# Two K pairs of the output projection's first half change places

## The chip, the cores and the metric

The kernel runs on one core of one Trainium2 chip. The metric is the device time of one execution in microseconds (us), as the median of the runs; lower is better. TensorE (PE) multiplies matrices and loads its stationary operand in a separate instruction (PEld), VectorE (DVE) and ScalarE (ACT) do the elementwise work, GpSimd (POOL) helps in a few places, and SyncE (SP) issues most of the DMAs. PSUM has eight banks of 128x512 f32 in which matmuls add up.

## The reference, cut to what matters

Two layers, 256 tokens, width 2048. Each layer has a mixer and a SwiGLU block, both with a norm ahead and a norm behind and a residual. The mixer has two groups of eight heads, whose outputs stand side by side and go through one output projection:

```python
o_sb = stick_breaking_attention(q_sb, k_sb, v_sb)      # heads 0 to 7
o_sb = rms_norm(o_sb, sb_out_norm)
...
o_d = differential_attention(q1, q2, k1, k2, v_d, lam) # heads 8 to 15
o_d = rms_norm(o_d, diff_subln) * (1.0 - lam_init)
mix = jnp.concatenate([o_sb.reshape(b, s, SB_WIDTH), o_d.reshape(b, s, DIFF_V_WIDTH)], axis=-1)
return mix @ w_o
```

`mix` is 256 x 2048 and `w_o` is 2048 x 2048. The sum over the 2048 rows of `w_o` may be taken in any order.

## The kernel before, in words

**Splitting.** Every f32 operand is split into a rounded part `hi` and the rest `lo`. A product of two split operands is three matmuls, hi x hi, hi x lo and lo x hi, of 128x128 by 128x512, which all add into one PSUM bank (lines 629 to 631). ACT makes `hi` of a weight tile (line 330), DVE makes `lo` (line 340). A ring of six `hi` and six `lo` buffers holds the split weights, and a ring of four `raw` buffers holds what the DMA has brought (512 KB each).

**The weight stream.** All weights are laid out in DRAM in the order in which they are used, by `weight_order()`. Each entry is a tile of two K tiles (a "K pair", 256 rows of the weight) by 512 columns (a "column" c). SP fetches the entries in that order, and ACT and DVE split them four entries ahead of their use.

**The output projection.** K pair kp covers heads 2kp and 2kp+1: pairs 0 to 3 are the stick-breaking heads, pairs 4 to 7 the differential ones. Columns 0 and 1 are the first half, columns 2 and 3 the second. The first half takes the K pairs in the order `KP_O`, both columns of a pair behind each other:

```python
KP_O = (4, 5, 6, 7, 0, 1, 2, 3)                                      # line 34
order_o = [(c, kp) for kp in KP_O for c in (0, 1)]                   # line 108
...
for n, (c, kp) in enumerate(units[6:]):                              # line 1296
    ...
    run_until(lambda: mixed >= {2 * kp, 2 * kp + 1})                 # line 1303
    unit({t: accs[c, t] for t in range(NT)}, mix, ..., kp, ...)      # line 1304
```

Pairs 4 and 5 go through a form with seven products instead of eight (`sevens_alone`, line 1293), with pair 6 woven between; pair 7 and pairs 0 to 3 are plain `unit`s. One unit is one entry of the weight stream: two K tiles by two token halves by three matmuls, 12 matmuls. Behind the seven products, `pool.end_of_sums()` (line 1294) frees the room in which the stick-breaking results are later put.

**The attention beside it.** The attention is written as generators which run beside the projections. `tick()` advances a counter and lets every generator whose turn has come issue its next stage; a plain `yield` sleeps two ticks, `yield 1` one. Each `unit` ticks twice, once ahead of each of its K tiles. `run_until(done)` ticks without issuing any unit until `done` holds. Stick-breaking heads come in two groups of four heads; group 0 fills K pairs 0 and 1, group 1 fills pairs 2 and 3. `attend()` (line 744) goes through one group, two heads at a time: it multiplies the weights with the values (lines 758 to 760, PSUM tile `o_sb`), two ticks later it takes squares (line 710), two ticks later it normalizes into `on` (line 715), and after four more ticks it transposes `on` on PE (line 729, tile `oT_ps`, four transposes, two per head) and ACT and DVE write the split result `mix` (lines 731 and 734); then the heads enter the set `mixed`. Only one group may be between its products and its `on` at a time (`attending`), so that the two groups take turns: heads 0 and 1, heads 4 and 5, heads 2 and 3, heads 6 and 7. The transposes want one of three shared PSUM banks, and those of stick-breaking heads wait for `end_of_sums`.

**What sets the order of the queues.** The program issues in the order in which the code runs, and that order is a priority. A planner at compile time then makes each engine's queue from the priorities and its own estimate of when the operands are there: where an instruction is not ready by that estimate, a later one that is ready goes ahead. On the chip the queues run in the planned order.

**Behind it.** The second half takes columns 2 and 3 in the order `LATE_O` (pair 6 first, then pair 4 through the seven products with weights in buffers `V`), then a part in an order written out by hand leads into the SwiGLU block (PE tile `c`), which is most of the time.

Of the kernel before, what the change touches and what calls it, by code (L numbers as in the profile page):

```python
# [30 lines left out]
DEFER_ACT = 7  # L31
URGENT = 50
TAIL = 3
KP_O = (4, 5, 6, 7, 0, 1, 2, 3)
LATE_O = (6, 4, 0, 1, 5, 2)
LAST_O = (3, 7)
O_SEVEN = (4, 5)
# [51 lines left out]
def weight_order():  # L89
# [9 lines left out]
    for l in range(L):  # L99
# [7 lines left out]
        aside[lay["in"][PAIRS[-1][1], IN_LAST[1]]] = "v"  # L107
        order_o = [(c, kp) for kp in KP_O for c in (0, 1)]
        order_o += [(c, kp) for kp in LATE_O for c in (2, 3)] + [(c, kp) for c in (2, 3) for kp in LAST_O]
        lay["order_o"] = order_o  # L110
        for c, kp in order_o:
            lay["o"][c, kp] = queue_pair("w_o", l, kp, c)
            if c == 3 and kp in O_SEVEN:
                own.add(lay["o"][c, kp])
            if c == 1 and kp in KP_O[:2]:
                plain.add(lay["o"][c, kp])
        aside[lay["o"][1, KP_O[1]]] = "sums"
        for c in range(FF // CW):
# [61 lines left out]
def kernel(  # L180
# [435 lines left out]
    def run_until(done):  # L616
        while not done():
            tick()
# [396 lines left out]
    def mixer_in(pool, l, rs, xT, mix, mixed):  # L1015
# [7 lines left out]
        for n, cc in enumerate(PAIRS):  # L1023
# [60 lines left out]
            else:  # L1084
# [3 lines left out]
                if alone:  # L1088
# [9 lines left out]
                    kps = kps[3:]  # L1098
                    ahead = list(KP_O[:2])
                for j, kp in enumerate(kps):  # L1100
# [166 lines left out]
    for l in range(L):  # L1267
# [18 lines left out]
        units = plan[l]["order_o"][:16]  # L1286
        run_until(lambda: mixed >= {2 * kp + j for kp in KP_O[:3] for j in range(2)})

# [3 lines left out]

        sevens_alone(got, forms, mix, KP_O[:2], [plan[l]["o"][c, kp] for c, kp in units[:4]], w, units_between)
        pool.end_of_sums()
# [406 lines left out]
```

## Time and profile before

| what | value |
|---|---|
| median of the runs | 2179.39 us |
| all runs | 2178.74, 2184.57, 2179.39 us |
| profiled execution, its own time | 2180.22 us |
| its span (first to last instruction) | 2178.5 us |
| mean granted TensorE clock | 0.999 |

The profiled execution is 0.83 us above the median, and its span is 1.7 us shorter than its time. All stamps below are us from the start of that span. A row of the timeline reads: start, duration, engine, line, operation, what it writes `<-` what it reads, shape, number, and in brackets how long the engine had been idle and what ended that. The names drop the numbers of the buffers, so `mix_sb` is the split result of any stick-breaking pair, `mix_df` that of any differential pair. The output projection's first half is at 296 to 349 us in layer 0 and at 1380 to 1433 us in layer 1.

### The profile page before, as it was taken

The page shows a single profiled execution, that of the slowest core. Times are in us where ns is not written, and L with a number is a line of the kernel's source. Part 1 is how long each engine was busy: PE and PEld are TensorE (multiplying, and loading weights), DVE is VectorE, ACT ScalarE, POOL GpSimd, SP SyncE. Part 2 cuts the span into 40 slices and gives each one's busy share as a digit, 9 for nine tenths or more (in the row PEclk, how much of TensorE's full clock was granted, in tenths as well). Part 3 has the DMA queues.
Part 4 walks back from the last instruction along what each step waited for, and adds up shares of the span by engine and source line. Part 5 has one row for each costly group of instructions (what it writes and reads, how often), then busy time and mean ns, then how long its engine had stood idle before and what let it go on. Part 6 is the DMA issues. An engine that isn't in the chain of part 4 may idle for free.

```text
span 2178.5 us, 28781 instructions
## 1 busy us (share of the span) xinstructions
PE 2161.9 (99%) x9932; PEld 1778.3 (82%) x9932; DVE 1960.4 (90%) x2705; ACT 1414.4 (65%) x2113; POOL 246.5 (11%) x239
## 2 busy tenths in 40 slices
PE   9999999999999999999999999999999999999998
PEld 7888888888888888888878888888888888888886
DVE  7888977899999999999878888778999999999997
ACT  7666775765766666666665667757566666576664
POOL 2100000021221220000010000000212212200000
PEclk9999999999999999999999999999999999999999
DMA  8545446497887877767465564455978877767683
GB/s 324 194 165 200 161 171 199 156 307 230 248 260 225 232 234 233 224 228 253 146 242 174 179 206 155 171 179 184 294 232 253 257 224 237 232 218 241 203 269 99
DMA packets 140275, 470.44 MB, mean 216 GB/s; under 512 B 15952, under 2 KB 16976, under 8 KB 139616
## 3 DMA queue, kind: packets, MB, share of 16 engines
q1 hardware_dynamic: 121952, 436.03, 57.9%
q0 software_dynamic: 17600, 32.02, 8.9%
q8 instruction: 78, 1.28, 0.2%
q14 instruction: 69, 0.57, 0.1%
q10 hardware_dynamic: 576, 0.54, 0.1%
HBM read 460.14 MB, written 8.39 MB: 215 GB/s over the span
## 4 chain that ended last, share of the span: by engine, by line
PE 90%; DVE 5%; ACT 2%; DMA 2%; issue 2%; DVEq 0%; SPq 0%; ACTq 0%
PE c L1351 20%; PE in L1219 7%; PE in L1221 7%; PE in L1220 7%; PE dn L1582 4%; PE dn L1585 4%; PE dn L1583 4%; PE p L1220 3%; PE c L1219 2%; PE c L1220 2%; PE p L1221 2%; PE c L1221 2%; PE p L1219 2%; PE o L629 2%; PE o L631 2%; PE o L630 2%
## 5 line engine op out<-in xcount | busy, mean ns | idle before, releaser
L340 DVE TENSOR_TENSOR lo<-raw,hi 128x1024 fp32r<-128x1024 f32 x448 | 544.0, 1233 | 58.5 <-ACT hi L330 57.4
L330 ACT ACTIVATE hi<-raw 128x1024 fp32r<-128x1024 f32 x470 | 480.1, 1054 | 73.6 <-DMA raw<-in_weights_in_turn_dram 33.2
L1351 PE MATMUL c<-hi,xF 128*128 128x512 f32 x1344 | 364.4, 392 | 0.7 <-DVE xF L539 0.5
L1351 PEld LDWEIGHTS c<-hi,xF 128*128 128x128 f32 x1344 | 249.7, 188 | 53.3 <-ACT act L1469 1.9
L270 POOL DMA_DIRECT2D T<-in_weights_in_turn_dram x122 | 107.6, 882 | 1367.5 <-PE c L1351 541.0
L1351 PE MATMUL c<-lo,xF 128*128 128x512 f32 x672 | 207.4, 390 | 0.0
L302 ACT ACTIVATE Th<-T 128x512 fp32r<-128x512 f32 x122 | 77.2, 633 | 199.4 <-DVE T L313 198.4
L302 ACT ACTIVATE Th<-G 128x1024 fp32r<-128x1024 f32 x122 | 129.0, 1058 | 80.0 <-DVE G L314 78.6
L1582 PE MATMUL dn<-hi,jh 128*128 128x512 f32 x416 | 162.0, 389 | 0.0
L1583 PE MATMUL dn<-lo,jh 128*128 128x512 f32 x416 | 161.8, 389 | 0.0
L304 DVE TENSOR_TENSOR Tl<-G,Th 128x1024 fp32r<-128x1024 f32 x122 | 148.9, 1221 | 11.6 <-ACT Th L302 11.6
L304 DVE TENSOR_TENSOR lo<-T,hi 128x1024 fp32r<-128x1024 f32 x122 | 152.9, 1253 | 0.1
L330 ACT ACTIVATE hi<-G 128x1024 fp32r<-128x1024 f32 x122 | 128.9, 1056 | 36.5 <-DMA G<-in_weights_in_turn_dram 22.1
L314 DVE TENSOR_TENSOR G<-G,T 128x1024 f32<-128x1024 f32 x122 | 148.7, 1219 | 2.6 <-DVE T L313 0.9
L1351 PEld LDWEIGHTS c<-lo,xF 128*128 128x128 f32 x672 | 126.0, 188 | 26.4
L340 DVE TENSOR_TENSOR lo<-G,hi 128x1024 fp32r<-128x1024 f32 x104 | 126.8, 1219 | 10.1 <-ACT hi L330 9.9
L302 ACT ACTIVATE hi<-T 128x1024 fp32r<-128x1024 f32 x122 | 128.0, 1050 | 11.4 <-PE c L1221 8.3
L1585 PE MATMUL dn<-hi,jl 128*128 128x512 f32 x416 | 128.1, 389 | 0.0
L1219 PE MATMUL in<-hi,xT 128*128 128x512 f32 x316 | 125.9, 400 | 1.6 <-DVE xT L929 1.6
L1219 PE MATMUL in<-hi,xI 128*128 128x512 f32 x316 | 126.1, 400 | 0.0
L1220 PE MATMUL in<-lo,xI 128*128 128x512 f32 x316 | 123.5, 391 | 0.3 <-DVE lo L340 0.3
L1221 PE MATMUL in<-hi,xI 128*128 128x512 f32 x316 | 123.2, 391 | 0.0
(522 smaller groups left out, 5028.8 us busy)
## 6 DMA issues: line engine op xcount, KB each, us to landing
raw<-in_weights_in_turn_dram SPq DMA_DIRECT2D x482, 512.0 KB, 4.9
T<-in_weights_in_turn_dram SPq DMA_DIRECT2D x122, 512.0 KB, 5.3
G<-in_weights_in_turn_dram SPq DMA_DIRECT2D x122, 512.0 KB, 5.4
T<-in_weights_in_turn_dram POOLq DMA_DIRECT2D x122, 256.0 KB, 5.6
GU<-in_weights_in_turn_dram SPq DMA_DIRECT2D x48, 512.0 KB, 6.4
V<-in_weights_in_turn_dram SPq DMA_DIRECT2D x8, 512.0 KB, 5.3
away_ffn<-x SPq DMA_DIRECT2D x8, 512.0 KB, 7.2
xd<-away_ffn SPq DMA_DIRECT2D x8, 512.0 KB, 9.2
```

The lines of the kernel that those rows point to most:

```text
L302: nc.scalar.activation(h, w, AF.Copy)
L304: newest_rest[i] = nc.vector.tensor_tensor(out=l, in0=w, in1=h.bitcast(F32), op=ALU.subtract)
L314: nc.vector.tensor_tensor(out=g, in0=g, in1=t2.unsqueeze(1).to_broadcast([P, 2, CW]), op=ALU.add)
L330: nc.scalar.activation(hi, raw, AF.Copy)
L340: rest = nc.vector.tensor_tensor(out=lo, in0=raw, in1=hi.bitcast(F32), op=ALU.subtract)
L1219: nc.tensor.matmul(a, sh, hi, start=first, stop=False, skip_group_check=open_sums[0])
L1220: nc.tensor.matmul(a, sh, lo, start=False, stop=False, skip_group_check=open_sums[0])
L1221: return nc.tensor.matmul(a, sl, hi, start=False, stop=last, skip_group_check=open_sums[0])
L1351: nc.tensor.matmul(a, stat[part], w[j][:, kk, :], start=first and kk + n == 0, stop=last and kk == 1 and n == 2)
L1582: nc.tensor.matmul(accs[c, t], sh, hi[:, kk, :], start=first, stop=False, skip_group_check=open_sums[0])
L1583: nc.tensor.matmul(accs[c, t], sh, lo[:, kk, :], start=False, stop=False, skip_group_check=open_sums[0])
L1585: nc.tensor.matmul(accs[c, t], sl, hi[:, kk, :], start=False, stop=last, skip_group_check=open_sums[0])
```

## The change

K pairs 1 and 2 change places in `KP_O`:

```diff
-KP_O = (4, 5, 6, 7, 0, 1, 2, 3)
+KP_O = (4, 5, 6, 7, 0, 2, 1, 3)
```

`KP_O` is read in four ways. `weight_order()` lays out the weight stream by it, so the four entries of pairs 1 and 2 (two columns each) change places in DRAM too, in both layers. `units` (line 1286) is the same list. `KP_O[:2]` (pairs 4 and 5), `KP_O[:3]` (line 1287) and `KP_O[-1]` (pair 3, lines 1304 and 1305) are what they were. The order of the generators' stages and the second half's order are not touched.

## The prediction

> **What bounds the kernel now.** I read the totals of the page first, then TensorE's waits, then the stretches around the change, then the timeline of each engine there.
>
> ```profile
> span 2178.5 us, 28781 instructions
> PE 2161.9 (99%) x9932; PEld 1778.3 (82%) x9932; DVE 1960.4 (90%) x2705; ACT 1414.4 (65%) x2113; POOL 246.5 (11%) x239
> ...
> raw<-in_weights_in_turn_dram SPq DMA_DIRECT2D x482, 512.0 KB, 4.9
> ```
> ```profile
> PE p L1220 <- DVE Tl L304: 2.5, 3, 1.2
> ...
> PE oT_ps_sb L729 <- DVE on_sb L715: 1.5, 2, 0.9
> ```
> ```profile
> 330.00:350.00 20.00, 19.34 (x88) 15.61 (x87) 13.52 (x20) 9.13 (x15) 0.00 (x0) 1.00 0.59 203
> 1414.00:1434.00 20.00, 19.13 (x89) 15.56 (x88) 13.74 (x21) 9.48 (x15) 0.00 (x0) 1.00 0.58 203
> 540.00:700.00 160.00, 160.00 (x724) 132.71 (x722) 155.82 (x173) 106.88 (x122) 36.83 (x28) 1.00 0.82 248
> ```
>
> TensorE works for 2161.9 of 2178.5 us, so all its idle time together is 16.6 us. Of that, 1.5 us in two waits belongs to the output projection's first half, one in each layer: transposes of a stick-breaking result wait for `on`. The two stretches of 20 us hold nothing else that TensorE waits for (20 less 19.34 is 0.66, 20 less 19.13 is 0.87), VectorE is busy there for 13.5 and 13.7 us, ScalarE for 9.1 and 9.5. There TensorE alone sets the pace.
>
> The timeline of TensorE in layer 0 shows the place. A matmul's stamped duration overlaps the next, so prices are taken from start to start.
>
> ```profile
> 316.44 0.60 PE L729 MATMUL oT_ps_sb<-ident,on_sb 128*128 128x128 f32 x4
> 316.88 0.39 PE L758 MATMUL o_sb<-v,w_sb 128*128 128x128 f32 x2
> ...
> 320.73 0.39 PE L631 MATMUL o<-hi,mix_df 128*128 128x512 f32 x1
> 320.95 0.60 PE L729 MATMUL oT_ps_sb<-ident,on_sb 128*128 128x128 f32 x4
> 321.31 0.47 PE L629 MATMUL o<-hi,mix_df 128*128 128x512 f32 x1
> 321.62 0.39 PE L630 MATMUL o<-lo,mix_df 128*128 128x512 f32 x1
> ...
> 324.14 0.38 PE L758 MATMUL o_sb<-v,w_sb 128*128 128x128 f32 x2
> ...
> 330.70 0.39 PE L631 MATMUL o<-hi,mix_sb 128*128 128x512 f32 x1
> 330.94 0.60 PE L729 MATMUL oT_ps_sb<-ident,on_sb 128*128 128x128 f32 x4
> 332.13 0.41 PE L729 MATMUL oT_ps_sb<-ident,on_sb 128*128 128x128 f32 x2 [0.59 <-DVE on_sb L715]
> ...
> 336.85 0.38 PE L729 MATMUL oT_ps_sb<-ident,on_sb 128*128 128x128 f32 x2
> ...
> 340.52 0.39 PE L629 MATMUL o<-hi,mix_sb 128*128 128x512 f32 x1
> ...
> 349.36 0.39 PE L629 MATMUL o<-hi,mix_df 128*128 128x512 f32 x1
> ```
>
> I call the results A, B, C, D in the order in which their transposes appear: 316.44 (A), 320.95 (B), 330.94 (C), and D in two halves at 332.13 and 336.85. Counted in ticks from `end_of_sums` by the code: A's transposes and C's products come at tick 1 (316.44 and 316.88 stand together), B's transposes at tick 3, between the two units of pair 7, C's `on` and D's products at tick 5 (324.14), C's transposes and D's `on` at tick 9, D's transposes at tick 13. With the groups in turns A is pair 0, B pair 2, C pair 1, D pair 3. The units of pairs 7 and 0 use ticks 1 to 8. Their last matmul is at 330.70. Then the program wants pair 1, which is C, not yet in `mixed`: `run_until` issues tick 9 with no unit under it. TensorE transposes C, and all that stands ready next in its queue is C's own result, which ScalarE and VectorE have yet to write. The planner filled this hole with half of D's transposes, and D's `on` was not there:
>
> ```profile
> 320.80 0.69 DVE L715 TENSOR_TENSOR on_sb<-o_sb,ors_sb 128x512 f32<-128x512 f32 x1
> ...
> 323.12 0.48 DVE L734 SCALAR_TENSOR_TENSOR mix_sb<-oT_ps_sb,gains,mix_sb 128x256 fp32r<-128x256 f32 x1 [0.54 <-ACT mix_sb L731]
> ...
> 331.29 0.69 DVE L715 TENSOR_TENSOR on_sb<-o_sb,ors_sb 128x512 f32<-128x512 f32 x1
> ...
> 334.39 0.48 DVE L734 SCALAR_TENSOR_TENSOR mix_sb<-oT_ps_sb,gains,mix_sb 128x256 fp32r<-128x256 f32 x1 [0.55 <-ACT mix_sb L731]
> ...
> 340.89 0.48 DVE L734 SCALAR_TENSOR_TENSOR mix_sb<-oT_ps_sb,gains,mix_sb 128x256 fp32r<-128x256 f32 x1
> ```
>
> B, which is pair 2, was complete at 323.12 + 0.48 = 323.60, seven microseconds before the hole, and its 24 matmuls were queued behind pair 1.
>
> **The change part by part.** *The order on TensorE.* Pair 2's two units (24 matmuls) go ahead of pair 1's (24). The count stays. `run_until` finds pair 2 in `mixed` and issues nothing, so ticks 9 to 12 lie under pair 2's units and tick 13 under pair 1's first. C's transposes (tick 9) come at the same place as now, ahead of pair 2; D's (tick 13) come between pair 2 and pair 1. C's result then has pair 2's 24 matmuls to hide behind, and D's `on` (331.29 + 0.69 = 331.98) is there well before its transposes.
>
> *The sum for layer 0.* The 39 steps from 340.52 to 349.36 take 8.84 us, 0.2267 us a matmul. Four transposes between two matmuls cost what 320.73 to 321.62 takes, 0.89, less two steps of 0.2267: 0.44 us. From the last matmul of pair 0 to the first of the second half there are 73 steps and two groups of transposes: 73 x 0.2267 + 2 x 0.44 = 17.42 us. Now it takes 349.36 - 330.70 = 18.66 us. The gain is 1.24 us: the wait of 0.59, and the refilling behind it with D's transposes cut in two.
>
> ```profile
> 1414.33 0.39 PE L631 MATMUL o<-hi,mix_sb 128*128 128x512 f32 x1
> ...
> 1416.03 0.41 PE L729 MATMUL oT_ps_sb<-ident,on_sb 128*128 128x128 f32 x2 [0.87 <-DVE on_sb L715]
> ...
> 1433.01 0.39 PE L629 MATMUL o<-hi,mix_df 128*128 128x512 f32 x1
> ```
>
> *Layer 1* takes 1433.01 - 1414.33 = 18.68 us for the same work: 1.26 us. Together 2.50 us.
>
> *What is late next.* C is needed at 330.70 + 25 x 0.2267 + 2 x 0.44 = 337.25 and was complete at 334.39 + 0.48 = 334.87, 2.4 us earlier. D is needed for pair 3 at 330.70 + 49 x 0.2267 + 0.88 = 342.69; even as late as now, with its second half transposed at 336.85, it was complete at 340.89 + 0.48 = 341.37, 1.3 us earlier. In layer 1 the need is at 1426.32 by the same sum. If that cover were gone, TensorE would wait the difference.
>
> *The weights.* Four entries of the stream change places in each layer, with the same size (512 KB each), the same SP queue and the same number of `hi` and `lo`: nothing is added, and SP's other transfers keep their places. The cover is the lead of the splitting:
>
> ```profile
> 323.94 1.06 ACT L330 ACTIVATE hi<-raw 128x1024 fp32r<-128x1024 f32 x1 [0.85 <-DMA raw<-in_weights_in_turn_dram]
> ...
> 331.13 1.06 ACT L330 ACTIVATE hi<-raw 128x1024 fp32r<-128x1024 f32 x1 [1.51 <-PE o L631]
> ...
> 341.40 1.06 ACT L330 ACTIVATE hi<-V 128x1024 fp32r<-128x1024 f32 x1 [1.32 <-PE o L631]
> ...
> 344.40 1.06 ACT L302 ACTIVATE hi<-V 128x1024 fp32r<-128x1024 f32 x1 [1.94 <-DVE V L308]
> ```
>
> By the ring of six, the split at 323.94 is the second entry of the swapped four, used at 334 in either order; it did wait 0.85 us for its DMA, with some 9 us in hand. A landing, 4.9 us in the median, would have to come another 9 us later to reach TensorE. At 331.13 ScalarE waits for TensorE to free a buffer, so a TensorE that runs earlier pulls the splits after it. Zero.
>
> *Bounds.* The most the place can give is both transposes hidden in full: 18.66 - 73 x 0.2267 = 2.11, and 2.13 in layer 1, 4.24 together. The least is nothing, if VectorE takes the gain back later, or a loss, if D comes late (both below). I take 2.50, since the transposes' price comes from the same transposes some 10 us earlier. The profiled execution goes from 2180.22 to 2177.7 us, its span to 2176.0, and the median, 0.83 us under the profiled one, from 2179.39 to 2176.9.
>
> **The rivals.** *The gain is taken back (2179.4 us, 0.12).* In the SwiGLU columns VectorE is busy 155.82 of 160 us, and TensorE's largest group of waits, 2.5 us in all, is for VectorE. If the vector queue sets the pace from there on, TensorE only arrives earlier at the same wait. Against it: TensorE is busy all 160 of these 160 us, and VectorE's work there waits for buffers that TensorE frees, so it shifts along.
>
> The Trainium skill speaks for this rival: "Perfetto Trace Analysis", Identifying the Most-Contended Engine, says that matmul busy time does not tell how near TensorE is to its limit, that the busy share of weight loads does, and that the engine of the highest share is the one to improve. By that rule VectorE, at 90% against 82%, would be the bound and the sum would be zero. The trace does not bear it out here, by this row:
>
> ```profile
> L630 PEld LDWEIGHTS o<-lo,mix_sb x128: 187/188/192, 325.5 to 1473.6; 128*128 128x128 f32 x128
> ```
>
> One load of 188 ns in a step of 226.7 is 83%, so 82% is what a TensorE without gaps shows here.
>
> *The change doesn't do what it says (2179.4 us, 0.06).* The queue is planned, not the program's: the planner may already draw pair 2's matmuls ahead, or order the changed program so that D's first transposes stand early again. For it: it did move D's ahead of C's use. Against it: it did that where the program had a hole, and the hole goes.
>
> *The last pair comes late (2186.5 us, 0.18).* This one is slower than before. TensorE now reaches pair 3 some 1.2 us earlier, and D's transposes are issued behind pair 2. ScalarE's queue is in order; now D's two writes of `mix` stand ahead of the two splits of `V` at 341.40 and 344.40. If the planner puts them behind the second of these, they start at 344.40 + 1.06 = 345.46, and the chain of two writes on ScalarE and two on VectorE takes what A's took:
>
> ```profile
> 317.08 0.47 ACT L731 ACTIVATE mix_sb<-oT_ps_sb,gains 128x256 fp32r<-128x256 f32 x1 [0.74 <-PE oT_ps_sb L729]
> ...
> 318.61 0.48 DVE L734 SCALAR_TENSOR_TENSOR mix_sb<-oT_ps_sb,gains,mix_sb 128x256 fp32r<-128x256 f32 x1 [0.54 <-ACT mix_sb L731]
> ```
>
> That is 318.61 + 0.48 - 317.08 = 2.01 us, so D is complete at 347.47 where pair 3 wants it at 342.69: 4.78 us lost, 3.55 net of the gain, 7.1 in both layers. It decides from the point where the writes stand behind the second `V` split; behind the first alone, D comes at 341.40 + 1.06 + 2.01 = 344.47, 1.8 us lost, 0.5 net. For it: the planner's times were wrong about D once already (0.59 and 0.87 us). Against it: D's stages keep their priority ahead of the second half's weights.
>
> *Much faster (2172.7 us, 0.04).* If the transposes hide in full (4.24) and the shifted SwiGLU entry also loses the 2.5 us of waits for `Tl`, 6.7 us go. Nothing in the change touches the latter.
>
> **How the numbers follow.** 0.3% of 2179.39, about what a measurement of this kernel can tell from no change, is 6.5 us. The forecast, a gain of 2.5 us, gets 0.60; with the two cases of no gain that is 0.78 within 0.3%. The late pair has 0.18 and is slower by over 0.3%; much faster has 0.04. The range begins at 2174.5: the full 4.24 us from the median, 2175.15, less the 0.65 us by which the fastest run lies under it. It ends at 2184.0: the late pair in one layer alone gives 2179.39 + 3.55 - 1.26 = 2181.7, and the two other runs stood up to 5 us above the fastest, of which I allow 2.3. The forecast's own range is 2174.5 to 2178.5. Left out are both tails of the last two rivals, together about 0.2.
>
> **What would show it.** In the profile after, the group of waits of `oT_ps_sb` for `on_sb` is gone, pair 1's and pair 3's results are each transposed in one group of four with matmuls close on both sides, and 17.4 us lie between pair 0's last matmul and the second half's first, in both layers. TensorE's busy time hardly moves, its idle falls by 1.5 us. Wrong are: D's transposes ahead of pair 2's matmuls with a wait; a wait of line 629 or 631 for VectorE's `mix_sb` at pair 3; or a first half shorter by 1.2 us with new waits for `Tl` or `lo` in the SwiGLU columns of the same size.

## The result, and the profile after

| | before | after |
|---|---|---|
| median of 22 runs each | 2181.26 us | 2177.95 us |
| lowest to highest | 2178.52 to 2186.35 us | 2175.60 to 2179.84 us |
| profiled execution, its span | 2178.5 us | 2178.1 us |

The ratio after to before is 0.9984, with a 95% interval of 0.9977 to 0.9990: a gain of 3.5 us, between 2.2 and 5.0. The medians differ by 3.31 us. The profiled execution of after took 2179.84 us and is the slowest of its 22, so its span hides most of the gain; the place where the gain arises is read from the stamps.

Totals of the page after, and the head of TensorE's waits (us in total, times, longest):

```profile
span 2178.1 us, 28781 instructions
PE 2162.9 (99%) x9932; PEld 1779.2 (82%) x9932; DVE 1958.8 (90%) x2705; ACT 1413.3 (65%) x2113; POOL 247.0 (11%) x239
```
```profile
PE p L1220 <- DVE Tl L304: 2.1, 3, 1.1
PE xb_d L682 <- ACT r_d L681: 1.7, 1, 1.7
PE xT_ps L525 <- DVE xd L669: 1.3, 1, 1.3
```

The group of `oT_ps_sb` waiting for `on_sb`, 1.5 us before, would stand between the second and the third of these; it is gone, and further down there is no smaller one. TensorE's idle time is 2178.1 - 2162.9 = 15.2 us against 16.6. The same two stretches of 20 us (PE, PEld, DVE, ACT and POOL busy, granted clock, DMA share, GB/s) are now full:

```profile
330.00:350.00 20.00, 20.00 (x94) 16.56 (x93) 14.70 (x22) 10.07 (x16) 0.00 (x0) 1.00 0.57 203
1414.00:1434.00 20.00, 20.00 (x94) 16.56 (x93) 15.21 (x23) 10.51 (x17) 0.00 (x0) 1.00 0.60 213
```

TensorE's timeline there, first layer 0, then layer 1:

```profile
330.86 0.39 PE L631 MATMUL o<-hi,mix_sb 128*128 128x512 f32 x1
331.09 0.60 PE L729 MATMUL oT_ps_sb<-ident,on_sb 128*128 128x128 f32 x4
...
331.76 0.40 PE L630 MATMUL o<-lo,mix_sb 128*128 128x512 f32 x1
...
336.79 0.39 PE L631 MATMUL o<-hi,mix_sb 128*128 128x512 f32 x1
337.02 0.60 PE L729 MATMUL oT_ps_sb<-ident,on_sb 128*128 128x128 f32 x4
337.37 0.47 PE L629 MATMUL o<-hi,mix_sb 128*128 128x512 f32 x1
...
342.92 0.39 PE L629 MATMUL o<-hi,mix_sb 128*128 128x512 f32 x1
...
348.36 0.39 PE L629 MATMUL o<-hi,mix_df 128*128 128x512 f32 x1
...
1415.12 0.39 PE L631 MATMUL o<-hi,mix_sb 128*128 128x512 f32 x1
1415.35 0.60 PE L729 MATMUL oT_ps_sb<-ident,on_sb 128*128 128x128 f32 x4
...
1421.28 0.60 PE L729 MATMUL oT_ps_sb<-ident,on_sb 128*128 128x128 f32 x4
...
1432.63 0.39 PE L629 MATMUL o<-hi,mix_df 128*128 128x512 f32 x1
```

C (331.09) and D (337.02) are each transposed in one group of four, with pair 2's matmuls in between and pair 1's behind. I call the time from pair 0's last matmul to the second half's first one the *stage*. It is 348.36 - 330.86 = 17.50 us in layer 0 and 1432.63 - 1415.12 = 17.51 in layer 1, against 18.66 and 18.68: 1.16 and 1.17 us less, 2.33 together.

VectorE's and ScalarE's timelines of after, layer 0:

```profile
334.54 0.48 DVE L734 SCALAR_TENSOR_TENSOR mix_sb<-oT_ps_sb,gains,mix_sb 128x256 fp32r<-128x256 f32 x1 [0.54 <-ACT mix_sb L731]
...
340.47 0.48 DVE L734 SCALAR_TENSOR_TENSOR mix_sb<-oT_ps_sb,gains,mix_sb 128x256 fp32r<-128x256 f32 x1 [0.54 <-ACT mix_sb L731]
```
```profile
339.96 0.47 ACT L731 ACTIVATE mix_sb<-oT_ps_sb,gains 128x256 fp32r<-128x256 f32 x1 [1.32 <-DVE mix_sb L734]
340.40 1.06 ACT L330 ACTIVATE hi<-V 128x1024 fp32r<-128x1024 f32 x1
```

C is complete at 335.02 and its first matmul starts at 337.37; D is complete at 340.95 and pair 3 begins at 342.92. D's second write on ScalarE (339.96) stands ahead of the first split of `V` (340.40).

### The profile page after: what moved, and what is told of

Its sections match the earlier page's. It is cut to its first block, busy times and chain, and to the rows that moved or that the text cites. A ratio compares the mean times of both kernels' runs of the same rounds, so it can differ in the third digit from the quotient of the medians.

```text
span 2178.1 us, 28781 instructions
## 1 busy us (share of the span) xinstructions
PE 2162.9 (99%) x9932; PEld 1779.2 (82%) x9932; DVE 1958.8 (90%) x2705; ACT 1413.3 (65%) x2113; POOL 247.0 (11%) x239
## 4 chain that ended last, share of the span: by engine, by line
PE 91%; DVE 5%; issue 2%; ACT 1%; DMA 1%; DVEq 0%; SPq 0%; ACTq 0%
PE c L1351 20%; PE in L1219 6%; PE in L1221 6%; PE in L1220 6%; PE dn L1585 4%; PE dn L1583 4%; PE dn L1582 4%; PE p L1220 3%; PE c L1220 2%; PE c L1219 2%; PE p L1221 2%; PE c L1221 2%; PE p L1219 2%; PE o L631 2%; PE o L629 2%; PE o L630 2%
## 5 line engine op out<-in xcount | busy, mean ns | idle before, releaser
L1219 PE MATMUL in<-hi,xI 128*128 128x512 f32 x316 | 126.3, 401 | 0.0
L1220 PE MATMUL in<-lo,xT 128*128 128x512 f32 x316 | 123.4, 391 | 0.3 <-DVE lo L958 0.3
```

What stands on the lines that cost most here:

```text
L1219: nc.tensor.matmul(a, sh, hi, start=first, stop=False, skip_group_check=open_sums[0])
L1220: nc.tensor.matmul(a, sh, lo, start=False, stop=False, skip_group_check=open_sums[0])
```

## The experiments

Each ratio is to the kernel before, timed on the same chip in the same rounds, with its 95% interval. Stages are given as layer 0 / layer 1.

**One layer at a time.** The new order in layer 0 alone; the other kernel has `l == 1` at that place.

```diff
-order_o = [(c, kp) for kp in KP_O for c in (0, 1)]
+order_o = [(c, kp) for kp in ((4, 5, 6, 7, 0, 2, 1, 3) if l == 0 else KP_O) for c in (0, 1)]
```

> The new order in layer 0 alone, the old one in layer 1. Theory (the hole behind C's transposes is filled by pair 2's matmuls, and the gain reaches the end): from pair 0's last matmul to the second half's first 17.5 us in layer 0 and 18.7 in layer 1, the time 1.2 us less than before. Rival (VectorE takes the gain back in the SwiGLU block of layer 0, where the profile of the change shows the second column 1.2 us longer than before): 17.5 and 18.7 us as well, but the column between the first two groups of transposes of act takes 44.1 us instead of 42.9, and the time is that of before within 0.3 us.

> The new order in layer 1 alone. Theory: 18.7 us in layer 0, 17.5 in layer 1, the time 1.2 us less than before, so that this and the run with layer 0 alone add up to the change. Rival (layer 0's gain is taken back): this one has all of the change's gain, 2.5 to 3.5 us.

Layer 0 alone: stages 17.51 / 20.26 us, median 2179.08 against 2180.45, ratio 0.9996 [0.9987, 1.0005]. Layer 1 alone: 18.66 / 17.51, median 2178.51, ratio 0.9992 [0.9983, 1.0000]. The stage changes only where the order does. The two differences of medians, 1.37 and 1.94, add up to 3.31, that of the whole change; the exact agreement is chance, since each is uncertain by about 2 us. Neither interval by itself excludes no gain, and that of layer 1 alone, 0 to 3.7 us, does not decide against the rival by which it has all of the gain.

The 20.26 was not expected. In that kernel layer 1 is in the old order (timelines of TensorE, VectorE and ScalarE):

```profile
1414.08 0.60 PE L729 MATMUL oT_ps_sb<-ident,on_sb 128*128 128x128 f32 x4
1417.22 0.41 PE L729 MATMUL oT_ps_sb<-ident,on_sb 128*128 128x128 f32 x2 [2.54 <-DVE on_sb L715]
...
1434.10 0.39 PE L629 MATMUL o<-hi,mix_df 128*128 128x512 f32 x1
```
```profile
1416.38 0.69 DVE L715 TENSOR_TENSOR on_sb<-o_sb,ors_sb 128x512 f32<-128x512 f32 x1
```
```profile
1409.04 1.06 ACT L330 ACTIVATE hi<-raw 128x1024 fp32r<-128x1024 f32 x1 [2.81 <-DMA raw<-in_weights_in_turn_dram]
```

ScalarE's split of a weight waited 2.81 us for its DMA, and D's squares stand behind it in ScalarE's queue. Before, the same split waited less:

```profile
1407.84 1.06 ACT L330 ACTIVATE hi<-raw 128x1024 fp32r<-128x1024 f32 x1 [1.13 <-DMA raw<-in_weights_in_turn_dram]
```

D's `on` started 2.30 us behind C's transposes (1416.38 - 1414.08) instead of 0.63 (1415.19 - 1414.56): 1.67 later, and the DMA's wait is 1.68 longer. The stage grows with it, from 1.17 to 2.75 us above 17.51. With the new order in layer 1 alone, the same split waited nearly as long:

```profile
1410.15 1.06 ACT L330 ACTIVATE hi<-raw 128x1024 fp32r<-128x1024 f32 x1 [2.47 <-DMA raw<-in_weights_in_turn_dram]
```

There the stage stayed at 17.51. So the new order also made the stage indifferent to a landing as late as this.

**Pair 2 ahead of pair 0.** Is it the order of finishing that matters, or only what stands between C's transposes and C's use?

```diff
-KP_O = (4, 5, 6, 7, 0, 1, 2, 3)
+KP_O = (4, 5, 6, 7, 2, 0, 1, 3)
```

> Another order: pairs 2, 0, 1, 3, which is not that in which the attention finishes. C's transposes still come at tick 9, now with pair 0's 24 matmuls behind them instead of pair 2's. Theory (only what lies between C's transposes and C's use counts): 17.5 us in both layers, the same time as the change, 2.5 us less than before. Rival (the order of finishing counts): TensorE waits for pair 2's result ahead of its units, 18 us or more.

```profile
331.85 0.39 PE L631 MATMUL o<-hi,mix_sb 128*128 128x512 f32 x1
...
349.36 0.39 PE L629 MATMUL o<-hi,mix_df 128*128 128x512 f32 x1
```

From the matmul ahead of C's transposes to the second half: 17.51 / 17.51; median 2177.24, ratio 0.9987 [0.9978, 0.9996]. This order takes pair 2, the second to be finished, ahead of the first, and is as good. So the order of finishing did not matter here; 24 ready matmuls between C's transposes and C's use are enough for the whole gain in the stage.

**C transposed early, nothing moved.** The old order, with C's transposes two ticks earlier, between pair 0's two units.

```diff
-        yield
+        yield from (None,) * (0 if nm[0] == "s" and nm.endswith("_0_1") else 1)
```

> The old order of the pairs; C's transposes are issued two ticks earlier, between the two units of pair 0, so that 12 matmuls (2.7 us) lie between them and pair 1. Theory: the chain of C's writes takes some 2 us and is hidden by 2.7 us, so 17.4 to 17.7 us in both layers with no pair moved, and 2 to 2.5 us less time than before. Rival (the order of the pairs counts, or D's on): 18.1 us or more.

```profile
322.07 0.60 PE L729 MATMUL oT_ps_sb<-ident,on_sb 128*128 128x128 f32 x4
...
329.33 0.60 PE L729 MATMUL oT_ps_sb<-ident,on_sb 128*128 128x128 f32 x4
...
349.60 0.39 PE L629 MATMUL o<-hi,mix_df 128*128 128x512 f32 x1
```

Here pair 0's matmuls lie on both sides of C's transposes (329.33), so I measure from B's transposes (322.07) to the second half: 27.53 / 27.48 us, against 28.41 / 28.43 before and 27.25 / 27.26 after. That is 0.88 / 0.95 of the 1.16 / 1.17 us, without moving a pair, or a stage of 17.78 / 17.73 us: nearer to the expected 17.4 to 17.7 than to the rival's 18.1, but just outside. In layer 0, ScalarE's second write of C (333.70) stands behind the split of a weight (332.74), and two matmuls from 333.90 on take 0.65 us where two steps are 0.45. Median 2178.05, ratio 0.9992 [0.9983, 1.0001]: in the time alone it can't be told from no change.

**D held back.** Before's wait row names D's `on`. In the old order, D's transposes are issued behind the last matmul that the program has issued by then, that of the first K tile of pair 1's second unit, so that they can't fall into the hole.

```diff
-                nc.tensor.matmul(a, sl, hi[:, kk, :], ...)
+                last_mm[0] = nc.tensor.matmul(a, sl, hi[:, kk, :], ...)
...
-        for i in range(4):
-            nc.tensor.transpose(pb[:, i * P : (i + 1) * P], on[:, i, :], ident)
+        with tc.issue_after(last_mm[0].ins) if nm[0] == "s" and nm.endswith("_1_1") else nullcontext():
+            [nc.tensor.transpose(pb[:, i * P : (i + 1) * P], on[:, i, :], ident) for i in range(4)]
```

> The old order; D's four transposes are held behind the first matmuls of pair 1's second unit, so that nothing stands between C's transposes and C's matmuls. Theory (TensorE has to wait for C's result in any case, the wait for D's on lies inside that one): the wait for on is gone and one for mix at line 629 of 0.9 to 1.2 us stands in its place, 18.3 to 18.7 us in both layers, the time that of before. Rival (the wait for D's on is the cost): 18.07 us in layer 0 and 17.8 in layer 1, the wait of 0.59 and 0.87 less.

```profile
PE o L629 <- ACT mix_sb L731: 2.1, 2, 1.1
```
```profile
331.26 0.39 PE L631 MATMUL o<-hi,mix_sb 128*128 128x512 f32 x1
...
333.16 0.50 PE L629 MATMUL o<-hi,mix_sb 128*128 128x512 f32 x1 [1.07 <-ACT mix_sb L731]
...
350.11 0.39 PE L629 MATMUL o<-hi,mix_df 128*128 128x512 f32 x1
```

Stages 18.85 / 18.82, just over the expected 18.3 to 18.7 and far from the rival's 18.07 / 17.8; median 2180.55 against 2180.62, ratio 1.0002 [0.9992, 1.0012]. The wait for `on` is gone, and one of 1.07 us stands in its place in each layer: TensorE waits for the first written part of C. Two rows of before say the same once one knows what to look for. There, too, pair 1's first matmul starts just as ScalarE's first write of C ends (332.10 + 0.46 = 332.56):

```profile
332.10 0.46 ACT L731 ACTIVATE mix_sb<-oT_ps_sb,gains 128x256 fp32r<-128x256 f32 x1
```
```profile
332.61 0.50 PE L629 MATMUL o<-hi,mix_sb 128*128 128x512 f32 x1
```

So C's chain sets the hole here, and the wait for D's `on` lies inside it, unless `on` comes later. It did so by far in the 20.26 us stage, and slightly in layer 1 of a second profile of before (below): there C's first write ended at 1415.89, D's transposes waited 1.01 us for `on` until 1415.87, and pair 1 began at 1416.04.

Part of C's chain is ScalarE's queue. In layer 0 of before the write at 332.10 starts only when the split of a weight at 331.13 is through, 1.16 us behind C's transposes (330.94); A's write, with no split ahead of it, started 0.64 us behind its own (316.44 to 317.08).

**The last pair third.** The hole moved to D: pair 3 directly behind D's transposes, pair 1 last.

```diff
-KP_O = (4, 5, 6, 7, 0, 1, 2, 3)
+KP_O = (4, 5, 6, 7, 0, 2, 3, 1)
```

> Pairs 0, 2, 3, 1: the hole moves to D, whose transposes (tick 13) are now right ahead of D's own matmuls, with D's on complete long before. Theory (a hole stands wherever a pair's transposes are right ahead of its units): 18.0 to 18.7 us in both layers, with TensorE waiting for mix at line 629 instead of for on at line 729; half or all of the gain is gone. Rival (the wait was for D's on, and D's on is early here): 17.5 us in both layers.

```profile
336.18 0.60 PE L729 MATMUL oT_ps_sb<-ident,on_sb 128*128 128x128 f32 x4
336.54 0.47 PE L629 MATMUL o<-hi,mix_df 128*128 128x512 f32 x1
...
337.86 0.50 PE L629 MATMUL o<-hi,mix_sb 128*128 128x512 f32 x1
```

The expected wait did not come. The planner filled the hole with five matmuls of the second half (`mix_df`, from 336.54). From pair 0's last matmul (330.02) to the second half's sixth (348.93) it is 18.91 us, in layer 1 18.99. Less five steps of 0.2267 for the five inside, the stage is 17.78 / 17.86 us, 0.3 over that of after and between the two expectations. Median 2177.95 against 2180.62, ratio 0.9984 [0.9975, 0.9994]. Here the hole cost what the planner found nothing for, not the length of the chain.

**The loads of x later.** Between pair 7's two units the program also has SP load x and the gain for the residual. Are these loads the reason why weights land late here? They are issued four entries later, in the old and in the new order of pairs.

```diff
-            if n == 1:
+            if n == 5:
```

> The old order of heads, with the loads of x and gpost for the residual issued after four more fetches of weights in place of ahead of them. If those loads are what makes the raw weights land late for ScalarE's conversion of weights ahead of result D's squares, that wait (1.1 to 2.8 us in layer 1 so far) shrinks to under 0.5 us, and the stage from pair 0's last matmul to the second half comes out between 18.5 and 18.8 us in both layers, with no stretch towards 20. If the landing is late for another reason, the wait stays at 1 us or more and layer 1's stage stays somewhere from 18.7 to 20.3. In neither case does the stage fall to 17.5, since TensorE would still wait for the written result C. Time: that of the kernel before, within 3 us.

> The new order of heads with the same later loads of x and gpost. Both theories: the stage stays at 17.5 us in both layers, since nothing in it waits for result D any more, so the time is that of the changed kernel, 2 to 4 us under the kernel before. If the later loads of x and gpost hold up the residual behind the projection, the time rises by that wait; if they free the queue for the weights elsewhere, it falls below 2176.

ScalarE's timelines: the old order with later loads, then the new order with later loads:

```profile
333.11 0.47 ACT L731 ACTIVATE mix_sb<-oT_ps_sb,gains 128x256 fp32r<-128x256 f32 x1 [2.10 <-PE oT_ps_sb L729]
...
1417.55 1.06 ACT L330 ACTIVATE hi<-raw 128x1024 fp32r<-128x1024 f32 x1 [1.33 <-DMA raw<-in_weights_in_turn_dram]
...
1418.51 0.82 ACT L731 ACTIVATE mix_sb<-oT_ps_sb,gains 128x256 fp32r<-128x256 f32 x2
```
```profile
1418.01 1.06 ACT L330 ACTIVATE hi<-raw 128x1024 fp32r<-128x1024 f32 x1 [2.04 <-DMA raw<-in_weights_in_turn_dram]
```

The wait moved along with the loads, 9 to 11 us later, in both kernels and both layers (0.44 and 1.33 us in the old order, 1.10 and 2.04 in the new). So it belongs to these loads, and in single profiles it is not clearly shorter than before. In the old order D's `on` now came in time and all eight transposes stand together. In layer 1 C's second write stands behind the waiting split, and TensorE waits for it:

```profile
333.64 0.50 PE L629 MATMUL o<-hi,mix_sb 128*128 128x512 f32 x1
...
1414.88 0.39 PE L631 MATMUL o<-hi,mix_sb 128*128 128x512 f32 x1
1415.11 1.03 PE L729 MATMUL oT_ps_sb<-ident,on_sb 128*128 128x128 f32 x8
...
1419.02 0.50 PE L629 MATMUL o<-hi,mix_sb 128*128 128x512 f32 x1 [0.64 <-ACT mix_sb L731]
...
1433.82 0.39 PE L629 MATMUL o<-hi,mix_df 128*128 128x512 f32 x1
```

Stages 18.06 / 18.94, both outside the expected 18.5 to 18.8. In both layers no split of a weight stands ahead of C's first write any more, which starts 0.63 us behind the first transposes (332.48 in layer 0) instead of 1.16, and pair 1 begins 1.16 us behind them instead of 1.67. That makes up about 0.5 of the 0.60 us by which layer 0's stage is shorter than before; in layer 1 the new waits take it back. So nearly half of a hole of some 1.2 us was a weight's split standing ahead of C's write. Median 2179.88 against 2180.03, ratio 0.9996 [0.9987, 1.0005]. With the new order: 17.50 / 17.51, median 2176.91, ratio 0.9986 [0.9976, 0.9995], the same as after. No version tried beats the changed kernel by more than the runs can tell.

**Both kernels once more.** One profile each, to see what of the first pair of profiles repeats.

> The changed kernel once more, for a second trace of it. If VectorE takes layer 0's gain back for good, the second SwiGLU column of layer 0 takes 44.1 us again; if that was one execution's, 42.9.

> The kernel before once more, for a second trace of it: how far the same column differs between executions of one kernel. 42.9 us if it is a property of the kernel, anything up to 44 if not. The first half takes 18.7 us in both layers.

After: stages 17.50 / 17.51, span 2175.1 us. Before: 18.66 / 18.75, span 2177.0. The stages repeat within 0.07 us; the spans are 3.0 and 1.5 us shorter than in the first pair. Part of the 3.0 is in one SwiGLU column of layer 0, between two groups of `actT_ps` transposes. First after, then its second profile, then the kernel with the new order in layer 1 alone, whose layer 0 is in the old order:

```profile
478.50 1.03 PE L1468 MATMUL actT_ps<-ident,act 128*128 128x128 f32 x8
...
483.01 1.19 PE L1351 MATMUL c<-hi,xF 128*128 128x512 f32 x4 [0.66 <-ACT act L1469]
...
517.28 0.50 PE L1220 MATMUL p<-Tl,sh 128*128 128x512 f32 x1 [1.09 <-DVE Tl L304]
...
522.63 1.03 PE L1468 MATMUL actT_ps<-ident,act 128*128 128x128 f32 x8
```
```profile
478.68 1.03 PE L1468 MATMUL actT_ps<-ident,act 128*128 128x128 f32 x8
...
521.45 1.04 PE L1468 MATMUL actT_ps<-ident,act 128*128 128x128 f32 x8
```
```profile
484.46 1.19 PE L1351 MATMUL c<-hi,xF 128*128 128x512 f32 x4 [0.68 <-ACT act L1469]
```

The column took 44.13, 42.77 and 43.66 us, in before's second profile 42.65 and with the new order in layer 0 alone 43.52. Over the six profiles with pair 1 ahead of pair 2 in layer 0 it was 42.63 to 43.66 (mean 42.99), over the six with pair 2 ahead 42.69 to 44.13 (mean 43.14).

## Why the prediction was right, point by point

*The hole on TensorE.* Right in place and nearly in size: 1.16 and 1.17 us where 1.24 and 1.26 were predicted. The mis-sized term is the filled stage, 17.50 us where 73 steps and two groups of transposes were to give 17.42. The missing 0.08 us is spread: the 22 steps from 331.76 to 336.79 take 5.03 us where 22 of 0.2267 are 4.99, each of the two transitions over a group takes 0.90 us instead of 0.89, and the 47 steps behind D's group make up the rest. The prediction's sign for the whole span, idle time down by 1.5 us and busy time unmoved, does not add up to its own 2.50 us: in the 20 us stretch of layer 0 the idle time fell by only 0.66 us while the stage fell by 1.16, so stamped durations cover part of the hole.

*What ends the wait.* Here the prediction's step failed in part. It put the gain down to "the wait of 0.59, and the refilling behind it with D's transposes cut in two". Holding D back left the stage at 18.85 / 18.82: the hole is C's own chain (transposes, a weight's split in ScalarE's queue, ScalarE's write), and D's transposes only filled some of it. The sum did not suffer, since it was taken from both ends of the stage and not from the named wait.

*What is late next.* Nothing, as predicted. C is 337.37 - 335.02 = 2.35 us early (2.4 predicted), D 342.92 - 340.95 = 1.97 us (at least 1.3 predicted).

*The last pair comes late.* This rival needed D's writes behind a split of `V`; they stayed ahead of both. Even with pair 3 directly behind D's transposes the planner found other matmuls.

*The change doesn't do what it says.* It does. Before, TensorE paused behind C's transposes although pair 2 had been complete since 323.60, and went on as C's first write ended, so no matmul of pair 2 filled the hole; after, 24 matmuls stand there, and D's transposes behind them.

*The gain is taken back.* In the first profile it looks so: its column is 1.19 us longer than before's 42.94 (479.50 to 522.44), with 0.66 us of waits for `act` and 1.09 for `Tl`. The second profile of after has 42.77, and a kernel with the old order there shows the same wait for `act`. These lengths vary between profiles of one kernel; the means of the two orders differ by 0.15 us, less than either group's spread. A loss of some tenths of a us there is not excluded. Against the Trainium skill's rule ("Perfetto Trace Analysis", Identifying the Most-Contended Engine), by which VectorE at 90% would be the bound and the sum zero, the interval of the gain, 2.2 to 5.0 us, excludes zero.

*The size at the end.* The prediction had 2.50 us, the profiled stages give 2.33, the runs 3.5. The interval holds all of them. The time itself was put at 2176.9 us, 1.05 below the measured 2177.95, because the prediction started from a median of three runs that lay 1.87 us under that of the 22; that the two errors, of start and of gain, partly cancel is luck. (Of those three runs the slowest stood 5.83 us above the fastest, not "up to 5".) That the runs lie at the upper part has a likely reason, shown only in single profiles: the old order's stage in layer 1 stretches when the weights land late (18.68, 18.75, once 20.26 us), the new order's doesn't (17.51 in each of its profiles). How often executions stretch was not measured, so how much of the 1.2 us above 2.33 this explains stays open.

*The weights.* Costed at nothing, and rightly for the new order. For the old order the wait of 0.85 us for a landing in layer 0 was dismissed by its lead over the matmuls that use those weights. What it held up was not those matmuls but D's squares behind it in ScalarE's queue. That path was missing from the prediction.

## What to carry to other kernels

Where a result is transposed and written back by other engines before TensorE can use it, put ready matmuls between its transposes and its use; whose they were, and in which order the results were finished, did not matter here. Size such a hole from the last matmul ahead of it to a fixed matmul behind it, and not by the wait that the profile names: a planner's filler can make the named wait a bystander. And count what stands ahead of the write, and behind a late weight, in an engine's shared queue: a split of a weight ahead of the write was worth about 0.5 us of the hole here, and a schedule with slack also lost less when a transfer was late.

## What the runs showed of the hardware that was not expected

The landing of a 512 KB weight behind the loads of x and the gain varies between executions: ScalarE's wait for the same entry in layer 1 was 0.84, 1.13, 1.26, 1.61, 2.47 and 2.81 us in profiles whose queues differ only in pairs 1 and 2. In all six the wait began 7.61 to 7.62 us ahead of pair 0's last matmul, so it is its end, the landing, that varies. Moving those loads moved the wait and left it about as long (1.33 and 2.04 us).
